# Mean square of the differential heads: from two products over high and low part to one over half-rows

## The chip, the cores and the metric

The kernel runs on one core of a Trainium2 chip. The metric is the device time of one execution in microseconds, and less is better. A core has a matrix engine (TensorE, PE in the profile), a vector engine (VectorE, DVE), a scalar engine (ScalarE, ACT), a general engine (GpSimd, POOL) and a queue that issues most transfers (SyncE, SP). Each engine works through its own queue in order, and waits where an operand that another engine makes is not there yet.

## The reference

One decoder block on 528 positions (16 meta tokens and 512 tokens) of width 1024. After a LayerNorm, one projection of 10,240 columns feeds two attention branches of eight and sixteen heads, their gates and the merge gates. The edited part belongs to the differential branch. For each of its eight heads:

```python
a = p[:, :, 0] - lam * p[:, :, 1]                      # difference of two softmaxes
y = einsum('bhqk,bhkd->bhqd', a, v)                    # 128 channels for each query
xf * lax.rsqrt(jnp.mean(jnp.square(xf), axis=-1, keepdims=True) + RMS_EPS)   # RMS norm over them
```

The norm's result is scaled by the gain and by 0.8, multiplied by a SiLU gate, and goes on into the branch's output projection, the merge, the last projection and the closing LayerNorm.

## The kernel before

Everything is kept transposed: channels stand on the 128 partitions and the 512 tokens along the row. TensorE multiplies in a rounded 32-bit format (F32R). To stay near full precision, each operand is split in a high part (a copy rounded to F32R) and a low part (the rest, again F32R), and a product is taken as high by high, high by low and low by high. ScalarE makes most high parts, VectorE most low parts. A mean over the channels is a mean over partitions, which no vector pass can make, so it is a product with `onesm`, a 128 x 128 matrix whose every element is 1/128 (line 283). 1/128 has no low part, so the mean square takes two products: `onesm` by the high part of the squares and `onesm` by the low part.

The main loop (lines 969 to 1037) goes over 16 units: the eight differential heads, then eight pairs of stick-breaking heads. While one unit's attention runs, the next unit's keys and values and the one after's queries are projected (`proj_tok`, `proj_pos`, `stage_kv`). Each stretch of four input blocks of a weight is loaded, split in high (line 185, ScalarE) and low part (line 190, VectorE) by `prep`, four stretches ahead of the product that uses it, and held in six buffers.

A differential unit runs `d_scores` (scores, line 761; bias and minimum, 841; exponential, 845; difference, 851), then `transposed` (773, 778, 779), then `d_values`, whose products end with line 870. `d_values` also squares the attention output `av`, which lies in a PSUM bank of which there is one, and splits the squares. `d_norm`, called in the next unit at the due time 3.0 (5.8 after the last head; line 994), has the two products into a bank `ms` of the pool `ptp` (two banks, which the transposes use too), then Ln and Exp on ScalarE (lines 888 and 890, together the power -1/2), the multiplication with `av` and the gain on VectorE (893) and a store to DRAM (894). The buffers `sqh`, `sql` and `yd` come from the pool `gpool` under the tag `sg`, which has six buffers of 128 x 512 and is shared with the gates; `sq` and `r` share one buffer.

What sets the order: `run` calls the attention steps between the projection's parts by due times, so the code emits an order. Up to line 967 and from line 1041 on, `keep_order` ties each engine to the emitted order. In the main loop nothing is tied but a few single instructions (`placed`, `behind`, `follow`) and TensorE in the last unit: there the framework's planner sets the order on each engine. It simulates the program in time with its own costs (line 1270) and, where several instructions could go next on an engine, decides by that simulated time and the emitted order. On the chip the order is then fixed.

Of the kernel before, what the change touches and what calls it, by code (L numbers as in the profile page):

```python
# [9 lines left out]
F32 = mybir.dt.float32  # L10
F32R = mybir.dt.float32r
BF16 = mybir.dt.bfloat16
AF = mybir.ActivationFunctionType
ALU = mybir.AluOpType
PSUM = bass.MemoryType.PSUM

P = 128
D = 1024
KT = D // P
S = 512  # L20
# [22 lines left out]
LO, HI = slice(0, 64), slice(64, 128)  # L43
# [3 lines left out]
def hybrid_block_kernel(ctx: ExitStack, tc: tile.TileContext, x, meta, emb_g, emb_b, w_in, b_gate,  # L47
                        diff_lambda, subln_g, w_br_d, w_br_s, w_out, ln_g, ln_b, out):
    nc = tc.nc
    v, s, g, pe = nc.vector, nc.scalar, nc.gpsimd, nc.tensor  # L50
# [10 lines left out]
    gpool = ctx.enter_context(tc.tile_pool(name="g", bufs=6))  # L61
# [154 lines left out]
    def behind(name, on=True):  # L216

        if on:
            ins = nc.cur_bb.bb.instructions[-1]
            if name in state:  # L220
                follow(ins, state[name])
            state[name] = ins
# [22 lines left out]
    start = ExitStack()  # L245
# [37 lines left out]
    onesm = const.tile([P, P], F32R, name="onesm")  # L283
# [299 lines left out]
    with tc.tile_pool(name="att", bufs=1) as ap:  # L583
# [270 lines left out]
        def d_values(unit, ta):  # L854
            vh, vl = unit["V"]
            h, l = [v4[:, 2 * m:2 * m + 2].rearrange("p c d -> p (c d)") for m in range(2)]
            av = pav.tile([P, 512], F32, tag="av", name="av")
            unit["av"] = av
            pe.matmul(av, vh[:, 0, :], ta[0][0], start=True, stop=False)
            pe.matmul(av[:, 3 * P:], v3[:, 0:2].rearrange("p c d -> p (c d)"), ta[3], start=False, stop=False)  # L860
            ends = av.rearrange("p (i q) -> p i q", i=NB)[:, :, 96:]
            pe.matmul(ends, h, ta["strips"], start=False, stop=False)
            pe.matmul(ends, l, ta["strips"], start=False, stop=False)
            for j in range(1, 3):
                o = av[:, j * P:]
                pe.matmul(o, vh[:, j, :], ta[j][0], start=False, stop=False)
                pe.matmul(o, vh[:, j, :], ta[j][1], start=False, stop=False)
                pe.matmul(o, vl[:, j, :], ta[j][0], start=False, stop=False)
            pe.matmul(av, vh[:, 0, :], ta[0][1], start=False, stop=False)
            pe.matmul(av, vl[:, 0, :], ta[0][0], start=False, stop=True)  # L870
            sq = ap.tile([P, S], F32, tag="sq", name="sq")
            s.activation(sq, av, AF.Square)
            sqh = gpool.tile([P, S], F32R, tag="sg", name="sqh")
            sql = gpool.tile([P, S], F32R, tag="sg", name="sql")
            s.copy(sqh, sq)
            v.tensor_tensor(sql, sq, sqh.bitcast(F32), op=ALU.subtract)
            unit["sq"] = sqh, sql

        def d_norm(unit, h):
            av, sq = unit["av"], unit["sq"]  # L880
            ms = ptp.tile([P, 512], F32, tag="tp", name="ms")
            pe.matmul(ms, onesm, sq[0], start=True, stop=False)
            pe.matmul(ms, onesm, sq[1], start=False, stop=True)
            r = ap.tile([P, S], F32, tag="sq", name="r")
            if h == 7:
                s.preload_act_table_set("natural_log_exp_and_others")
                behind("act")
            s.activation(r, ms, AF.Ln, bias=epsr)
            behind("act", h == 7)
            s.activation(r, r, AF.Exp, scale=-0.5)  # L890
            behind("act", h == 7)
            y = gpool.tile([P, S], F32, tag="sg", name="yd")
            v.scalar_tensor_tensor(y, av, g08, r, op0=ALU.mult, op1=ALU.mult)
            nc.sync.dma_start(kept["d"][h], y)
# [74 lines left out]
        for u, (kind, n) in enumerate(UNITS):  # L969
            unit = units[u]  # L970
# [16 lines left out]
            if kind == "d":  # L987
# [3 lines left out]
                parts = transposed(ta, apads[n % 2])  # L991
                steps += [(t0 + 0.7 * m, f) for m, f in enumerate(parts)]
                steps.append((t1, lambda: d_values(unit, ta)))
                pending = [(3.0 if n < 7 else 5.8, lambda unit=unit, n=n: d_norm(unit, n))]
            else:
                if n == 0:
# [31 lines left out]
                for c in range(2):  # L1028
                    ta = {}
                    steps += spread(s_scores(unit, c, n == 0), (2.0 + 4.3 * c) if n == 0 else 4.4 * c, 0.85, 5)  # L1030
                    parts = transposed(ta, apads[c])
# [15 lines left out]
    def operands(y):  # L1047


        gh, gl = [lp.tile([P, 7, 4, 256], F32R, tag=n, name=n) for n in ("gh", "gl")]  # L1050

        def part(i):
            a, b = y[i], y[i + 4]
            t = lp.tile([P, 4, 256], F32, tag="tmp", name="t", bufs=2)
            v.tensor_tensor(t[:, 0, :], a[:, LEFT], a[:, RIGHT], op=ALU.subtract)
            v.tensor_tensor(t[:, 2, :], a[:, RIGHT], b[:, RIGHT], op=ALU.subtract)
            v.tensor_tensor(t[:, 1, :], t[:, 2, :], a[:, LEFT], op=ALU.subtract)
            v.tensor_tensor(t[:, 3, :], t[:, 1, :], b[:, LEFT], op=ALU.add)
            for o, src in ((slice(0, 1), a[:, LEFT].unsqueeze(1)), (slice(1, 3), b.rearrange("p (a n) -> p a n", a=2)),
                           (slice(3, 7), t)):  # L1060
                s.copy(gh[:, o, i, :], src)
                v.tensor_tensor(gl[:, o, i, :], src, gh[:, o, i, :].bitcast(F32), op=ALU.subtract)

        return (gh, gl), [lambda i=i: part(i) for i in range(4)]
# [40 lines left out]
    G, parts = operands(ydT)  # L1105
# [11 lines left out]
    G, parts = operands(ysT)  # L1117
# [75 lines left out]
    for c in range(2):  # L1193
        for t in range(NB):
            st, final = sts[t], t == NB - 1
            for o, w in [(0, 256), (256, 256)] if final and c else [(0, 512)]:
# [5 lines left out]
                for n, (k, (m, w)) in enumerate(products):  # L1202
                    pe.matmul(ps, MH[k][:, ts(t, P)] if m == "h" else ML[:, k, ts(t, P)], WO[c]["hl".index(w)][:, k, r],  # L1203
                              start=(n == 0), stop=(n == 3 * KT - 1))
# [70 lines left out]
```

## Time and profile before

| What | Value |
| --- | --- |
| Median of 3 runs | 706.76 us (706.19 to 706.91) |
| The profiled execution | 706.21 us |
| its span, first to last instruction | 704.4 us |
| TensorE busy | 694.8 us (99%) |
| VectorE busy | 569.9 us (81%) |
| ScalarE busy | 440.7 us (63%) |
| Mean granted TensorE clock | 0.997 |
| First product of the mean square (line 882) | x8, from 79.8 to 258.2 us |
| Second product (line 883) | x8, from 81.9 to 261.7 us |

A row of a time line gives the start in us from the span's start, the duration, the engine, the line of the code, the operation, what it writes and reads, and the shapes. In brackets at the end stands how long the engine had been idle and what ended that. A row of a group gives, behind the bar, the busy time in us, the mean duration of one in ns, and the idle time ahead of them. A row of waits names who waited for what: us in total, how often, the longest. Matmuls are pipelined, and their rows overlap.

### The profile page before, as it was taken

To read this page: it belongs to the slowest core of one execution; us is meant where nothing else is said; L and a number is where in the kernel's file an instruction comes from. 1 tells how busy PE (TensorE), PEld (TensorE's weight loads), DVE (VectorE), ACT (ScalarE), POOL (GpSimd) and SP (SyncE) were. 2 spreads that over 40 slices of the span, in tenths; PEclk is the share of its full clock that TensorE was granted. 3 is DMA by queue.
4 is the path that set the end of the run, shared out by engine and by line. 5 is a ranking of instruction groups with operands and counts; after the bars stand their busy time and mean duration, and the time that the engine had idled before them with its cause. 6 is when DMAs were issued, how large, how long until landed. Compare 5 with 4: busy or idle time off the path is not lost.

```text
span 704.4 us, 13288 instructions
## 1 busy us (share of the span) xinstructions
PE 694.8 (99%) x4482; PEld 635.4 (90%) x4482; DVE 569.9 (81%) x1224; ACT 440.7 (63%) x1071; POOL 131.2 (19%) x144
## 2 busy tenths in 40 slices
PE   9999999999999999999999999999999999999995
PEld 8999999989899898998989899988888998999885
DVE  6887998878786777989877998976666788688886
ACT  5776767767566687777767687766555456555400
POOL 3243112222222201212121220000012101230011
PEclk9999999999999999999999999999999999999998
DMA  9398557988987886899798976647476749697702
GB/s 290 96 197 185 148 115 180 212 177 181 219 189 171 204 191 186 171 220 209 204 192 220 201 158 187 168 119 239 145 168 128 154 122 245 128 186 190 264 33 102
DMA packets 184054, 124.93 MB, mean 177 GB/s; under 512 B 8961, under 2 KB 168098, under 8 KB 183986
## 3 DMA queue, kind: packets, MB, share of 16 engines
q1 hardware_dynamic: 147890, 102.84, 50.1%
q0 software_dynamic: 35776, 20.19, 22.8%
q10 hardware_dynamic: 320, 1.06, 0.4%
q8 instruction: 35, 0.57, 0.3%
q14 instruction: 33, 0.27, 0.1%
HBM read 93.54 MB, written 9.44 MB: 146 GB/s over the span
## 4 chain that ended last, share of the span: by engine, by line
PE 95%; ACT 2%; DVE 1%; DMA 1%; issue 0%; SPq 0%; DVEq 0%; POOL 0%; ACTq 0%
PE q L697 18%; PE ps L498 12%; PE ps L496 12%; PE ps L497 12%; PE q L1080 11%; PE pso L1203 6%; PE ps L512 6%; PE sc L761 6%; PE t L773 4%; PE bank L387 1%; PE tv L730 1%; DMA xt<-in_x_dram 1%; PE av L928 1%; PE av L929 1%; PE av L922 1%; PE av L923 1%
## 5 line engine op out<-in xcount | busy, mean ns | idle before, releaser
L497 PE MATMUL ps<-hTl,w 128*128 128x512 f32 x368 | 144.7, 393 | 0.0
L190 DVE TENSOR_TENSOR w<-raw,w 128x512 fp32r<-128x512 f32 x168 | 114.4, 689 | 37.3 <-ACT w L185 36.5
L496 PE MATMUL ps<-hTh,w 128*128 128x512 f32 x368 | 144.6, 393 | 0.0
L498 PE MATMUL ps<-hTh,w 128*128 128x512 f32 x368 | 144.6, 393 | 0.0
L185 ACT CAST w<-raw 128x512 fp32r<-128x512 f32 x168 | 103.4, 627 | 11.7 <-PE ps L498 5.4
L147 POOL DMA_DIRECT2D rawk<-in_w_in_dram x48 | 66.1, 1631 | 121.6 <-DMA rawk<-in_w_in_dram 55.2
L697 PE MATMUL q<-tS,w 128*128 128x264 f32 x384 | 82.5, 289 | 0.0
L1080 PE MATMUL q<-gh,w 128*128 128x256 f32 x448 | 81.4, 283 | 0.2 <-ACT t L1089 0.2
L498 PEld LDWEIGHTS ps<-hTh,w 128*128 128x128 f32 x368 | 69.2, 188 | 13.6
L497 PEld LDWEIGHTS ps<-hTl,w 128*128 128x128 f32 x368 | 69.2, 188 | 13.1
L496 PEld LDWEIGHTS ps<-hTh,w 128*128 128x128 f32 x368 | 69.2, 188 | 13.0
L1080 PEld LDWEIGHTS q<-gh,w 128*128 128x128 f32 x448 | 70.1, 192 | 0.5 <-ACT t L1089 0.4
L761 PE MATMUL sc<-k,A 128*128 128x264 f32 (+3 forms) x320 | 65.8, 298 | 0.0
L697 PEld LDWEIGHTS q<-tS,w 128*128 128x128 f32 x384 | 63.6, 188 | 0.3
L1080 PE MATMUL q<-gl,w 128*128 128x256 f32 x224 | 63.4, 283 | 0.0
L697 PE MATMUL q<-hTh,w 128*128 128x264 f32 x288 | 60.8, 286 | 0.0
L913 DVE TENSOR_TENSOR_SCAN e<-e,diag 128x528 f32<-128x528 f32 (+1 forms) x64 | 54.2, 851 | 5.6 <-ACT e L907 5.6
L697 PE MATMUL q<-tl,w 128*128 128x264 f32 x192 | 54.8, 286 | 0.0
L761 PEld LDWEIGHTS sc<-k,A 128*128 128x128 f32 x320 | 50.1, 189 | 2.1
L512 PE MATMUL ps<-hTh,w 128*128 128x264 f32 x256 | 51.5, 288 | 0.2 <-ACT k L639 0.2
L697 PEld LDWEIGHTS q<-hTh,w 128*128 128x128 f32 x288 | 47.7, 189 | 1.0 <-DVE kvt L717 0.2
L778 ACT CAST ah<-t 128x384 fp32r<-128x384 f32 (+2 forms) x72 | 34.4, 478 | 22.4 <-PE t L773 22.3
(283 smaller groups left out, 1576.0 us busy)
## 6 DMA issues: line engine op xcount, KB each, us to landing
raw<-in_w_in_dram SPq DMA_DIRECT2D x140, 256.0 KB, 3.5
rawk<-in_w_in_dram POOLq DMA_DIRECT2D x48, 256.0 KB, 5.9
rawk<-in_w_in_dram SPq DMA_DIRECT2D x36, 256.0 KB, 3.7
k<-ks SPq DMA_DIRECT2D x60, 132.0 KB, 3.2
raw<-in_w_out_dram SPq DMA_DIRECT2D x16, 256.0 KB, 3.0
k<-ks SPq DMA_DIRECT2D x60, 66.0 KB, 3.2
A<-low SPq DMA_DIRECT2D x28, 128.0 KB, 2.4
raw<-in_w_br_diff_dram SPq DMA_DIRECT2D x12, 256.0 KB, 5.1
```

Source lines behind the costliest of these rows:

```text
L147: second[l] = [lambda raw=raw, x=x: g.dma_start(raw, x, accum_op=ALU.add) for x in more]
L185: s.copy(wh, raw)
L190: eng.tensor_tensor(wl, raw, wh.bitcast(F32), op=ALU.subtract)
L496: pe.matmul(ps, wh[:, k % 4, :], hTh[:, k, M:], start=(k == 0), stop=False)
L497: pe.matmul(ps, wh[:, k % 4, :], hTl[:, k, M:], start=False, stop=False)
L498: pe.matmul(ps, wl[:, k % 4, :], hTh[:, k, M:], start=False, stop=(k == KT - 1))
L512: pe.matmul(ps[:, :H2], a[:, k % 4, :], b[:, k, ts(c, H2)], start=(k == 0 and m == 0), stop=(k == KT - 1 and m == 2))
L697: pe.matmul(bank, a[:, k, :], b, start=start and k == 0 and j == 0, stop=k == 3 and j == 2, skip_group_check=not start)
L761: pe.matmul(ps[:, :n], q, K[:, m, k0:k0 + n], start=(m == 0), stop=(m == 1))
L913: v.tensor_tensor_scan(rev, rev, diag[0][:, L - nk:][:, ::-1], 0.0, ALU.mult, ALU.max)
L1080: pe.matmul(bank, a[:, k, :], b[:, n, k, :], start=start and k == 0 and m == 0, stop=k == 3 and m == 2, skip_group_check=not start)
L1203: pe.matmul(ps, MH[k][:, ts(t, P)] if m == "h" else ML[:, k, ts(t, P)], WO[c]["hl".index(w)][:, k, r], start=(n == 0), stop=(n == 3 * KT - 1))
```

## The change

The mean over 128 channels is the sum over the lower 64 partitions plus the sum over the upper 64, divided by 128. The new code squares both halves separately, each as a pass over 64 partitions: the lower half into `sq[LO]`, the upper half, moved to the lower partitions, into `half[LO]`. VectorE adds the two. The sums fill only 64 partitions, so their high part and their low part fit into one tile: ScalarE writes the high part into the lower partitions of `parts`, VectorE the low part into the upper ones. One product of `onesm` with that tile adds up all 128 partitions, and so high and low parts together. `d_norm` has one product in place of two. The rest of `d_norm`, its due times and all other code stay.

```diff
-            s.activation(sq, av, AF.Square)
-            sqh = gpool.tile([P, S], F32R, tag="sg", name="sqh")
-            sql = gpool.tile([P, S], F32R, tag="sg", name="sql")
-            s.copy(sqh, sq)
-            v.tensor_tensor(sql, sq, sqh.bitcast(F32), op=ALU.subtract)
-            unit["sq"] = sqh, sql
+            s.activation(sq[LO], av[LO], AF.Square)
+            half = gpool.tile([P, S], F32, tag="sg", name="half")
+            s.activation(half[LO], av[HI], AF.Square)
+            v.tensor_tensor(sq[LO], sq[LO], half[LO], op=ALU.add)
+            parts = gpool.tile([P, S], F32R, tag="sg", name="parts")
+            s.copy(parts[LO], sq[LO])
+            v.tensor_tensor(parts[HI], sq[LO], parts[LO].bitcast(F32), op=ALU.subtract)
+            unit["sq"] = parts
...
-            pe.matmul(ms, onesm, sq[0], start=True, stop=False)
-            pe.matmul(ms, onesm, sq[1], start=False, stop=True)
+            pe.matmul(ms, onesm, sq, start=True, stop=True)
```

## The prediction

> **What bounds the kernel now.** I read the page's busy shares first, then the waits of TensorE, then the stretches, and last the time line around the edited lines.
>
> ```profile
> span 704.4 us, 13288 instructions
> PE 694.8 (99%) x4482; PEld 635.4 (90%) x4482; DVE 569.9 (81%) x1224; ACT 440.7 (63%) x1071; POOL 131.2 (19%) x144
> ```
>
> ```profile
> PE warm L308 <- POOL ident masks.py:199: 1.4, 1, 1.4
> PE bank L341 <- DVE xn L337: 0.2, 1, 0.2
> PE ps L512 <- ACT k L639: 0.2, 1, 0.2
> PE q L1080 <- ACT t L1089: 0.2, 1, 0.2
> ```
>
> ```profile
> 72.00:260.00 188.00, 188.00 (x1268) 174.71 (x1267) 156.25 (x422) 132.09 (x340) 40.49 (x39) 1.00 0.81 180
> ```
>
> The second block lists every wait of TensorE that the view shows in the whole span: us in total, how often, the longest. They come to 2.0 us. The third is the stretch in which all eight differential heads are normed: length, then busy us (and instructions) of PE, PEld, DVE, ACT and POOL, then granted clock, DMA share, GB/s. TensorE is busy for all 188.00 us at clock 1.00, VectorE for 156.25 (83%), ScalarE for 132.09 (70%). So TensorE sets the end, and what leaves its queue should come off the total, unless it is made to wait. What it then gains is not the busy time of a matmul, since a busy row runs into the next one:
>
> ```profile
> 79.61 0.40 PE L496 MATMUL ps<-hTh,w 128*128 128x512 f32 x1
> 79.84 0.39 PE L882 MATMUL ms<-sqh,onesm 128*128 128x512 f32 x1
> 80.07 0.39 PE L497 MATMUL ps<-hTl,w 128*128 128x512 f32 x1
> ...
> 81.66 0.40 PE L498 MATMUL ps<-hTh,w 128*128 128x512 f32 x1
> 81.89 0.39 PE L883 MATMUL ms<-sql,onesm 128*128 128x512 f32 x1
> 82.12 0.39 PE L496 MATMUL ps<-hTh,w 128*128 128x512 f32 x1
> ```
>
> The columns are start and duration. Each of these products is shown as 0.39 us, but the next one starts 0.23 us behind it (81.89 to 82.12). 0.23 us is the place in the queue that a removed product gives back; 0.39 is the length of its pipeline. The rows also show that the two products of one head, emitted one behind the other in the code, stand 2.05 us apart with projection products between: in the main loop the order on TensorE is the planner's.
>
> **The change part by part.** (a) The second product of the mean square (L883) goes, with its weight load, in each of eight heads. By 0.23 us each that is 8 x 0.23 = 1.84 us. By the busy time it would be 8 x 0.39 = 3.1 us, and I reject that: it counts the overlap with the following product twice. The lower bound is nothing, if some other engine becomes the bound; I take 1.84 us, since the rows show the pitch on both sides of both products. The Trainium skill, on the page "TensorE: Matmul & The Clock Gate", section "Back-to-back issue gap", says that in a real stream of weight loads and products one of 512 columns costs about 131 ns, not the isolated 216 ns; the sum would then be 8 x 0.131 = 1.05 us. The 0.23 us between the rows above speaks against it here.
>
> (b) ScalarE gets a third pass per head. The passes and VectorE's now:
>
> ```profile
> L872 ACT ACTIVATE sq<-av 128x512 f32<-128x512 f32 x8 | 4.8, 597 | 4.7 <-PE av L870 4.6
> L875 ACT CAST sqh<-sq 128x512 fp32r<-128x512 f32 x8 | 5.1, 640 | 0.0
> L876 DVE TENSOR_TENSOR sql<-sq,sqh 128x512 fp32r<-128x512 f32 x8 | 6.0, 748 | 0.0
> L935 ACT COPY half<-av 64x512 f32<-64x512 f32 x16 | 9.3, 582 | 12.2 <-PE av L930 8.5 <-issue 2.6 <-ACT e L909 0.9
> L538 ACT COPY gr<-ps 128x512 f32<-128x512 f32 x6 | 3.5, 588 | 0.0
> L353 DVE SCALAR_TENSOR_TENSOR A<-bank,A 64x512 fp32r<-64x512 f32 x4 | 2.8, 690 | 1.8 <-ACT A L349 1.7
> L170 DVE TENSOR_TENSOR rawk<-rawk,raw 128x512 f32<-128x512 f32 x12 | 8.2, 684 | 0.0
> ```
>
> Columns behind the bar: busy us, mean ns of one, idle before. A copy of 64 partitions takes 582 ns against 588 for 128 of them, so halving the height saves nothing: two half Squares cost 2 x 0.59 instead of 0.60, and the cast stays at about 0.64. ScalarE: +0.59 us a head, 4.7 us in all. (c) VectorE gets one addition per head: 0.69 us by L170 and L353 (684 and 690 ns, full and half height), 5.5 us in all; the subtraction stays one of 512 columns. In the 188 us stretch that lifts VectorE from 156.25 to 161.8 and ScalarE from 132.09 to 136.8, against about 186.2 for TensorE then. Both stay below TensorE, so I cost them at nothing. What covers them is that weights are prepared ahead:
>
> ```profile
> ACT w L185 <- PE ps L498: 18.2, 22, 2.1
> ```
>
> ScalarE's weight casts wait for TensorE to give a weight buffer back, 22 times and up to 2.1 us: it is ahead of TensorE, as far as its buffers let it. If that cover went, the price is bounded by 4.7 + 5.5 = 10.2 us when every added pass lay on TensorE's path; nothing in the rows comes near that, since TensorE doesn't wait at all there.
>
> (d) The chain from the attention product to the mean square becomes longer. Before it is Square, cast, subtraction; now Square, Square, addition, cast, subtraction, with three changes of engine instead of one. The first head and the sixth, seventh and eighth, before:
>
> ```profile
> 73.85 0.39 PE L870 MATMUL av<-ah,V 128*128 128x512 f32 x1
> 74.28 0.60 ACT L872 ACTIVATE sq<-av 128x512 f32<-128x512 f32 x1
> 74.78 0.47 ACT L738 CAST V<-tv 128x384 fp32r<-128x384 f32 x1
> ...
> 75.30 0.64 ACT L875 CAST sqh<-sq 128x512 fp32r<-128x512 f32 x1
> ...
> 76.37 0.69 DVE L876 TENSOR_TENSOR sql<-sq,sqh 128x512 fp32r<-128x512 f32 x1
> ```
>
> ```profile
> 199.09 0.68 DVE L876 TENSOR_TENSOR sql<-sq,sqh 128x512 fp32r<-128x512 f32 x1
> 199.75 0.44 PE L882 MATMUL ms<-sqh,onesm 128*128 128x512 f32 x1
> 200.02 0.40 PE L883 MATMUL ms<-sql,onesm 128*128 128x512 f32 x1
> 200.26 0.30 PE L697 MATMUL q<-hTh,w 128*128 128x264 f32 x1
> ```
>
> ```profile
> 227.15 0.68 DVE L876 TENSOR_TENSOR sql<-sq,sqh 128x512 fp32r<-128x512 f32 x1
> 227.81 0.44 PE L882 MATMUL ms<-sqh,onesm 128*128 128x512 f32 x1
> 228.09 0.39 PE L883 MATMUL ms<-sql,onesm 128*128 128x512 f32 x1
> ```
>
> ```profile
> 257.12 0.68 DVE L876 TENSOR_TENSOR sql<-sq,sqh 128x512 fp32r<-128x512 f32 x1
> 258.24 0.39 PE L882 MATMUL ms<-sqh,onesm 128*128 128x512 f32 x1
> ```
>
> In the first head the cast ends at 75.94 and the subtraction starts 0.43 us later: that is what a change of engine costs with the work that is queued between. On ScalarE the next pass starts 0.50 us behind the Square (74.28 to 74.78). By these durations the first head's new chain would run: second Square 74.78 to 75.38, addition 75.81 to 76.50, cast 76.93 to 77.57, subtraction 78.00 to 78.69, with 0.43 us at each change. It ended at 77.06, so it becomes 1.6 us longer. Bounds: with nothing queued at the three changes 77.40, or 0.35 us longer; with 0.86 us at each 79.98, or 2.9 us. I take 1.6, since every engine's queue goes on holding the same other work. In the first head the low part was there at 77.06 and L883 starts at 81.89; 1.6 us more are hidden in those 4.83 us. In the sixth and seventh it is there at 199.77 and 227.83, and L883 starts 0.25 and 0.26 us later: no cover. The product must stand further back there, about 201.4 and 229.4, and TensorE must have something else to do until then. The cast now waits for VectorE's addition; behind it in ScalarE's queue stand the next head's exponentials, projections' evacuations and weight casts, for which VectorE and TensorE wait in turn. Since the planner draws the order anew with the changed passes in it, I take it that it puts the product where it reckons the operand ready, as it did when it set the pair of the first head 2.05 us apart, with both operands there long before. Its cost for TensorE I take as 0.05 us per head at most, 0 in the forecast: in the sixth head the two products now stand at 0.27 and 0.24 us instead of 0.23, so about 0.05 us of wait is in the kernel before already, and may go as well. From below, a loss: waits as in the rivals. From above, a gain of 8 x 0.05 = 0.4 us on top.
>
> (e) The bank of the mean square is held from one product to the Ln, not from the first of two; `parts` is one buffer of the gate pool where two were held until the products, and `half` is free after the addition. That eases two rotations; TensorE waits for neither now, so nothing comes of it. DMAs are untouched: no issue is moved or added, only the store of the normed head follows the chain.
>
> Sum: -1.84 + 0 + 0 + 0 = -1.84 us. The profiled execution took 706.21 us, its span 704.4 with 1.8 us around it, and would take 704.4. It stands 0.55 us below the median of the three runs, 706.76, against which the comparison goes: 706.76 - 1.84 = 704.9 us, 0.26% less. About 0.2%, 1.41 us, is what a measurement of this kernel can tell from no change, so the line lies at 705.35, and the forecast is only 0.4 us on the near side of it.
>
> **The rivals.** *The gain is eaten or smaller (within 0.2%).* TensorE waits a little at the new place of the product: 0.4 to 3.2 us in all eight heads together, 0.05 to 0.4 each. For it: the two heads without cover; if the planner kept L883's place there, TensorE would wait 1.6 - 0.25 = 1.35 us in each, 2.7 in all, and the time is 706.76 - 1.84 + 2.7 = 707.6. Against it: the planner places by readiness. Typical: 1 us of waits, 705.9. The skill's 131 ns ("TensorE: Matmul & The Clock Gate") would land in this case too, at 705.7, without any wait.
>
> *Slower: the product stands in the queue ahead of its operand.* TensorE takes its queue in order, so one product whose operand is late holds all products behind it. If the planner reckons the longer chain shorter than it is, and keeps the place of the first of the pair, TensorE waits 199.77 + 1.6 - 199.75 = 1.6 us in the sixth head, 1.6 in the seventh and 257.80 + 1.6 - 258.24 = 1.2 in the eighth: 4.4 us, and the time is 706.76 - 1.84 + 4.4 = 709.3 (with the bounds of 0.35 and 2.9 us for the chain 705.7 and 713.2). It decides from 0.4 us a head on, 3.25 us in all (1.84 + 1.41). For it: sub-0.3 us margins in these heads. Against it: in the first head the planner was late rather than early, and TensorE has not one listed wait between 72 and 260 us.
>
> *TensorE isn't the bound, the change shows nothing.* The 5.5 us of additions fall on VectorE at its busiest, which then feeds scores and transposes late; each head would lose about what it gains: 706.8. Against it: VectorE at 83%.
>
> **How the numbers follow.** The forecast, 704.3 to 705.35 us: 0.50. Gain eaten, within 0.2% (with the bound on VectorE): 0.29. Slower by the product in its place: 0.21. So faster by over 0.2% 0.50, within 0.29, slower 0.21. The predicted time is the forecast's 704.9. The range goes down to 703.8, which is the forecast with 0.4 us of present waits gone and 0.7 for a luckier order, and up to 708.6, which takes in the rival with 2.7 us of waits and the beginning of the slower one; about 0.18 is left out, two thirds of it above.
>
> **What would show it.** Right: 8 products fewer on TensorE and a pitch of 0.23 us around the one that is left, no new row in TensorE's list of waits between 72 and 260 us, a span of about 702.6, half-height Squares at 0.58 to 0.60 us each, an addition at 0.69, and the stretch from the first head's attention product to the last norm shorter by nearly 2 us with the tail unchanged. Wrong: starts around the mean square's product over 0.3 us apart; the product less than 0.1 us behind the end of the low part in more than two heads, with a gap ahead of it; or a new wait of TensorE elsewhere, on scores, transposes or weight splits, which would mean that the new order and not the product decides.

## The result, and the profile after

The changed kernel takes 712.71 us (median of 5 runs, 712.45 to 714.14), the kernel before 706.74 in the same comparison: ratio 1.009, with a 95% interval of 1.0079 to 1.0101. It is about 6 us slower, above the predicted range (703.8 to 708.6), where 704.9 was forecast.

The page of the changed kernel, its span and busy shares:

```profile
span 710.7 us, 13289 instructions
...
PE 696.6 (98%) x4474; PEld 636.0 (89%) x4474; DVE 576.3 (81%) x1232; ACT 446.1 (63%) x1079; POOL 133.0 (19%) x144
```

TensorE has 8 instructions fewer, as it should, and the span is 6.3 us longer. VectorE gained 6.4 us and ScalarE 5.4; neither is near the span. (In the code after, the passes stand at lines 872, 874, 875, 877 and 878, the product at 884, Ln at 889; other lines of this part are one further down.)

The stretches, first of the changed kernel, then the second one of the kernel before (columns as in the prediction: length, busy us of PE, PEld, DVE, ACT, POOL with counts, clock, DMA share, GB/s):

```profile
72.00:260.00 188.00, 186.51 (x1254) 173.14 (x1253) 162.06 (x429) 137.36 (x346) 42.44 (x39) 1.00 0.81 182
260.00:476.00 216.00, 212.84 (x1352) 193.12 (x1350) 178.42 (x334) 152.85 (x399) 34.24 (x30) 0.99 0.79 184
```

```profile
260.00:476.00 216.00, 216.00 (x1374) 195.95 (x1373) 182.84 (x343) 156.10 (x409) 35.06 (x31) 1.00 0.79 187
```

Where the edited code runs TensorE is idle for 1.5 us of 188; behind it, where not a line was changed, for 3.2 us of 216, and before for none. What it waited for, in the whole span (us in total, how often, the longest):

```profile
PE sc L761 <- issue: 2.3, 1, 2.3
...
PE ps L496 <- DVE kvt L714: 0.9, 1, 0.9
PE q L697 <- ACT gr L538: 0.5, 1, 0.5
PE av L923 <- ACT ys L940: 0.4, 1, 0.4
```

No row names the mean square's product. The largest is a wait of scores (L761) of a stick-breaking pair. To close the sum I took the starts of all TensorE rows, gave each shape the median distance to the next start, and added up what the distances over 60 ns more than that come to:

| From TensorE's first start to its last, us | before | after |
| --- | --- | --- |
| The instructions at their median distances | 683.97 | 682.06 |
| Longer distances, 0 to 240 us | 10.24 | 10.64 |
| 240 to 280 us | 0.52 | 2.48 |
| 280 to 320 us | 0.69 | 4.77 |
| 320 to 480 us | 2.88 | 5.06 |
| 480 us to the end | 1.29 | 1.20 |
| All other differences from the median | -4.46 | -4.31 |
| In all | 695.13 | 701.90 |

The products that are gone gave 1.91 us back, and two thirds of it had arrived at the seventh head, whose last attention product (L870) starts at 223.42 instead of 224.71. The loss comes behind that, in single waits, above all around 310 us.

The place around 310 us, on SyncE (first six rows) and on TensorE of the changed kernel, then SyncE of the kernel before:

```profile
300.63 1.49 SPq L621 DMA_DIRECT2D A<-A  x1
302.21 0.56 SPq L621 DMA_DIRECT2D A<-low  x1
302.87 0.54 SPq L556 DMA_DIRECT2D gd<-yd  x1
307.15 0.46 SPq L621 DMA_DIRECT2D A<-low  x1
307.70 0.55 SPq L651 DMA_DIRECT2D k<-ks  x1
...
310.30 1.28 SPq L650 DMA_DIRECT2D k<-ks  x2
...
309.96 0.60 PE L773 MATMUL t<-ident,apad 128*128 128x128 f32 x4
312.83 0.48 PE L761 MATMUL sc<-k,A 128*128 128x264 f32 x2 [2.27 <-issue]
```

```profile
303.79 1.28 SPq L650 DMA_DIRECT2D k<-ks  x2
305.17 0.56 SPq L621 DMA_DIRECT2D A<-A  x1
305.82 0.66 SPq L621 DMA_DIRECT2D A<-low  x1
```

`k<-ks` are the stores that bring a new unit's keys into place (lines 650 and 651); `A<-A` and `A<-low` assemble the queries of a later unit (line 621). Before, the keys' stores stand ahead of the query transfers in SyncE's queue. Now the query transfers stand in front. The third of them overwrites what the first reads, so it waits until the first has landed, and the six stores behind it in the queue go out late. SyncE's own list of waits between 280 and 320 us has it:

```profile
SPq L621 <- DMA A<-A: 3.7, 1, 3.7
```

The stores go out at 307.70 to 311.58 us, and the scores that read those keys start at 312.83.

The second place, at 256 us, on ScalarE, VectorE and TensorE of the changed kernel:

```profile
253.07 1.28 ACT L887 ACT_TABLE_LOAD   x1
254.37 0.59 ACT L872 ACTIVATE sq<-av 64x512 f32<-64x512 f32 x1
254.98 0.59 ACT L874 ACTIVATE half<-av 64x512 f32<-64x512 f32 x1
...
255.61 0.68 DVE L875 TENSOR_TENSOR sq<-sq,half 64x512 f32<-64x512 f32 x1 [0.46 <-ACT half L874]
...
256.88 0.41 DVE L714 TENSOR_TENSOR kvt<-q,kvt 128x264 f32<-128x264 f32 x1
...
257.35 0.50 PE L496 MATMUL ps<-hTh,w 128*128 128x512 f32 x1 [0.92 <-DVE kvt L714]
```

In the eighth head the load of the activation table now stands ahead of the Squares (before, it stood behind the Square, at 255.13). They come late, VectorE idles for the addition, and behind the addition stands the evacuation L714, the pass that reads out the bank which TensorE needs. Both places point to order: no operation there is longer than it was, though the second has a Square and an addition more.

### The profile page after: what moved, and what is told of

It reads as the page before. It is cut to its first block, busy times and chain, and to the rows that moved or that the text cites. A ratio compares the mean times of both kernels' runs of the same rounds, so it can differ in the third digit from the quotient of the medians.

```text
span 710.7 us, 13289 instructions
## 1 busy us (share of the span) xinstructions
PE 696.6 (98%) x4474; PEld 636.0 (89%) x4474; DVE 576.3 (81%) x1232; ACT 446.1 (63%) x1079; POOL 133.0 (19%) x144
## 4 chain that ended last, share of the span: by engine, by line
PE 86%; ACT 5%; DVE 4%; issue 3%; DMA 1%; POOL 0%; DVEq 0%; SPq 0%; ACTq 0%; POOLq 0%
PE q L697 14%; PE ps L496 11%; PE ps L497 11%; PE ps L498 11%; PE q L1081 11%; PE pso L1204 6%; PE ps L512 6%; PE sc L761 5%; PE t L773 3%; PE bank L387 1%; DVE w L190 1%; PE tv L730 1%; ACT w L185 1%; PE av L929 1%; PE av L930 1%
## 5 line engine op out<-in xcount | busy, mean ns | idle before, releaser
L761 PE MATMUL sc<-k,A 128*128 128x264 f32 (+3 forms) x320 | 67.1, 301 | 2.3 <-issue 2.3
L761 PEld LDWEIGHTS sc<-k,A 128*128 128x128 f32 x320 | 49.9, 189 | 4.9 <-issue 2.5
L941 POOL DMA_DIRECT2D ys<-half x14 | 11.7, 838 | 200.1 <-ACT ys L940 98.7
```

The source lines that it names most:

```text
L761: pe.matmul(ps[:, :n], q, K[:, m, k0:k0 + n], start=(m == 0), stop=(m == 1))
```

## The experiments

Each is compared with the kernel before on the same chip (706.3 to 706.7 us there). Where an order is said to be that of another kernel, a table of instruction numbers for each engine and queue ties each instruction to the one ahead of it, which sets the planner aside. In 1 to 5 the table stands at the top, so that the lines are 61 to 64 higher than in the kernel it comes from; in 13 it stands at the end.

**1. The new passes in the old order.** All operations of the change; every queue as in the kernel before; VectorE's two passes ahead of where the subtraction was, the product at L883's place.

```diff
+    for steps_ in given.values():
+        at, old = 0, None
+        for d in steps_:
+            at += d
+            new = named[f"I-{at}"]
+            if old is not None:
+                follow(new, old)
+            old = new
```

> The changed passes, with the order on all five queues written out as the planner set it for the kernel before: each second Square right behind the first, the addition two instructions ahead of the subtraction, the one product where the second of the pair stood (in the eighth head right ahead of the next transposes). If the new order is what costs (theory O): 706.7 - 1.84 + 2.7 us for the product standing 1.35 us too early in the sixth and seventh head = 707.6, and no wait of TensorE on scores near 310 us. If the added passes themselves cost, whatever the order (theory W): 711 to 713.

Measured: 708.56 us, ratio 1.0031 (1.0021 to 1.0041). Its waits of TensorE in the edited region, and VectorE in the sixth head:

```profile
PE ms L945 <- DVE parts L939: 1.2, 2, 0.6
...
PE q L758 <- ACT gr L599: 0.8, 1, 0.8
```

```profile
199.95 0.68 DVE L939 TENSOR_TENSOR parts<-sq,parts 64x512 fp32r<-64x512 f32 x1
200.67 0.43 DVE L778 TENSOR_TENSOR vT<-kvt,q 128x264 f32<-128x264 f32 x1
```

Where a price is given "by the distances", it is the time between two starts beyond the median, as in the table above; the view's waits are shorter. In the sixth and seventh heads the product waits for the low part, about 0.8 us each by the distances, and the next projections 0.23 more, since L778 (717 in the kernel before), which frees their bank, starts at 200.67 instead of 199.69. In the fifth head the cast holds an evacuation (L599, 538 before) back on ScalarE, 0.95 us. In all, the longer distances between 160 and 240 us grow by 3.3 us. So with the order kept the passes cost more than the product gives. 708.56 is 3.7 us above 706.68 - 1.84; the changed kernel is 7.8 us above the same kind of sum. The longer chain has a price of its own where the order was made for the shorter one, and that is less than half of what happened.

**2. The same with the product 12 matmuls further back** in the first to seventh heads. The edit is another table.

> As the run before it, but the product stands twelve matmuls further back (1.5 to 2.7 us), so that the longer chain is covered. Theory O: 704.9 to 705.6, that is the gain forecast. Theory W: 711 to 713.

Measured: 709.78 us, ratio 1.0042 (1.0027 to 1.0057): a miss. The product no longer waits, the projections behind do:

```profile
PE q L758 <- DVE vT L778: 1.1, 1, 1.1
PE q L758 <- DVE kvt L778: 1.1, 1, 1.1
```

With the product out of the way, the evacuation that stands behind the two new passes on VectorE ends last. It was there all the time, hidden by the product's wait. Moving the product alone gives nothing back. (That 2 is above 1 is mostly a wait of 0.7 us at 495 us, far behind the edit; the two intervals overlap.)

**3. The old passes in the new order.** The code of before, its instructions in the order that the changed kernel has, the two products next to each other at the one's place.

> The passes of the kernel before (one Square, cast, subtraction, two products), with the order on all queues as the planner set it for the changed kernel; the cast stands in the place of the second Square and in the first four heads the subtraction stands three to five instructions further ahead, because a buffer's turn asks for it; the pair stands where the one product stood. Theory O: 712.7 + 1.84 less about 1.1 us for the eighth head, where no addition holds VectorE any more: 712 to 714.5, slower than before although its passes are the same. Theory W: 706.7 to 707.5.

Measured: 713.73 us, ratio 1.0097 (1.008 to 1.0114). Without one new pass, and with both products, the kernel is 7.0 us slower than before and has the changed kernel's largest waits:

```profile
PE sc L825 <- DMA k<-ks: 2.6, 1, 2.6
...
PE ps L560 <- DVE kvt L778: 0.7, 1, 0.7
PE q L761 <- ACT gr L602: 0.5, 1, 0.5
```

L825 is 761: the scores wait for the keys' stores, and here the view names them. The order alone makes the kernel slow, whether the old work is done in it or the new. Two smaller waits of the changed kernel, at 226 and 250 us, 0.4 and 0.5 us by the distances, are down to 0.13 and 0.15 us here: these two come with the passes.

**4. The changed kernel with the keys' stores ahead of the query transfers.** Ten entries of SyncE's queue are put as before; all other queues keep the changed kernel's order. By lines, the queue becomes:

```diff
- L621 L621 L556 L621 L651 L650 L651 L651 L650 L650
+ L651 L556 L650 L651 L651 L650 L650 L621 L621 L621
```

> The changed kernel in its own order, but for ten neighbouring entries of SyncE's queue: the six stores of the second stick-breaking unit's keys stand ahead of the three transfers of a later unit's queries, as in the kernel before. If the wait of 2.3 us on the scores at 310 us comes from the third query transfer, which waits for the first and holds the keys' stores behind it: that wait is gone and 712.7 - 2.3 = 710.4. If something else holds the scores: 712.7, unchanged.

Measured: 708.83 us, ratio 1.0027 (1.0016 to 1.0038). That is 3.9 us less than the changed kernel, more than the 2.3 expected: the longer distances between 280 and 320 us fall from 4.77 to 0.77 us, so those behind the wait (about 1 us at 314 to 317 us) came from it too. Nearly two thirds of the loss of 6 us hang on these ten entries.

**5. And the table load behind the eighth head's passes as well.** ScalarE's queue, by lines, the other passes between them left out:

```diff
- L887 L872 L874 L877
+ L872 L874 L877 L887
```

> The changed kernel with its planner's order, in which two places are put as in the kernel before: the ten entries of SyncE's queue (keys' stores ahead of query transfers), and the table load that stands ahead of the eighth head's Squares on ScalarE, which goes behind the head's passes. Theory (the wait of 1.08 us of the key projections at 256 us comes from the table load, which delays the Squares, the addition and the evacuation behind it on VectorE): 708.83 less about 1.1, 707.7, and no wait for an evacuation (kvt, L714) near 256 us. Rival (that wait belongs to the longer chain itself, as in the sixth and seventh heads under the old order): 708.8, the wait still there or at the mean square's product. Seen beside 712.7 for the changed kernel and 706.5 for the kernel before.

Measured: 708.06 us, ratio 1.0021 (1.0012 to 1.003). The wait is half as long (0.53 instead of 1.08 us by the distances), and 0.8 us of the expected 1.1 come back (0.6 against the kernel before of each comparison; the intervals of 4 and 5 overlap, so the trace carries this more than the times):

```profile
PE ps L560 <- DVE kvt L778: 0.4, 1, 0.4
```

The addition now starts at 255.14 with VectorE busy up to it, and the evacuation at 256.41 instead of 256.88. So the table load is about half of that wait. What the other half hangs on was not separated; 3, which has no addition there, still waits 0.7 us. The rest of the loss is in smaller waits whose causes I did not take apart. By the distances the changed kernel has them at 226 us (0.4 us), 250 (0.5), 381 (0.7) and 475 to 477 (1.4 in three).

**6. One product alone.** The kernel before without L883. The low part is left out of the mean, so it shows what the product's place is worth, and is no version to use.

```diff
-            pe.matmul(ms, onesm, sq[0], start=True, stop=False)
-            pe.matmul(ms, onesm, sq[1], start=False, stop=True)
+            pe.matmul(ms, onesm, sq[0], start=True, stop=True)
```

> The kernel before with the second product of each mean square left out, so that the low part of the squares does not enter the mean (this leaves out that part of the computation); all passes as before, order left to the planner. If a removed product gives back its pitch of 0.23 us: 706.7 - 8 x 0.23 = 704.9. If the product was worth nothing there: 706.7; by the busy time of 0.39 us it would be 703.6.

Measured: 709.23 us (707.67 to 711.62), ratio 1.0038 (1.0023 to 1.0053): a miss on the other side. Work is taken away, nothing is added, and the kernel is slower. SyncE, TensorE's wait, and SyncE's longest wait between 325 and 342 us:

```profile
320.77 8.24 SPq L145 DMA_DIRECT2D raw<-in_w_in_dram  x3
...
330.62 0.47 SPq L621 DMA_DIRECT2D A<-A  x1
...
334.42 0.53 SPq L621 DMA_DIRECT2D A<-low  x1
...
337.14 0.58 SPq L621 DMA_DIRECT2D A<-low  x1
...
338.17 1.28 SPq L650 DMA_DIRECT2D k<-ks  x2
```

```profile
PE sc L761 <- DMA k<-ks: 1.7, 1, 1.7
```

```profile
SPq L145 <- DVE w L190: 6.3, 1, 6.3
```

In the next stick-breaking unit, too, query transfers stand between the keys' stores, the last two of which go out from 338.17 on, and the scores wait. But no query transfer is listed as waiting for the landing of another here. What held the queue longest was a weight load (L145): three stand ahead of the stores (the row of 8.24 us), where the kernel before has two, and the third waits 6.3 us for VectorE to give its buffer back. The kernel before has all its stores there first:

```profile
328.57 1.44 SPq L651 DMA_DIRECT2D k<-ks  x2
...
335.26 0.51 SPq L621 DMA_DIRECT2D A<-A  x1
```

**7. The passes alone.** The kernel before, with a half Square and a half addition into a buffer that nothing reads.

```diff
+            spare = gpool.tile([P, S], F32, tag="sg", name="spare")
+            s.activation(spare[LO], av[HI], AF.Square)
+            v.tensor_tensor(spare[LO], sq[LO], spare[LO], op=ALU.add)
```

> The kernel before with a second half-height Square and a half-height addition added in each head, into a buffer that nothing reads; cast, subtraction and both products stay, order left to the planner. Theory O (only the new order costs, and it comes from the longer chain that the product waits for): 706.7 to 707.2. Theory W (the added passes hold VectorE and ScalarE where TensorE depends on them): 708.7 to 710.5, with waits of TensorE near 172, 200 and 229 us.

Measured: 711.84 us, ratio 1.0073 (1.0049 to 1.0096). Its two largest new waits are again the keys' stores (in the same unit as in 6, behind the same weight load), and the mean square's product in the eighth head:

```profile
PE sc L761 <- DMA k<-ks: 2.4, 1, 2.4
...
PE ms L885 <- DVE v L751: 0.7, 1, 0.7
```

**8, 9, 10. One product alone, the passes alone, and the whole change, with one rule for SyncE:** a query transfer follows the eight keys' stores that the code emitted last ahead of it. The planner sets everything else.

```diff
                 nc.sync.dma_start(o.bitcast(F32), src.bitcast(F32))
+                for key in state.get("keys", []):
+                    follow(nc.cur_bb.bb.instructions[-1], key)
...
             staged.clear()
+            state["keys"] = [i for i in nc.cur_bb.bb.instructions[-8:] if i.engine == mybir.EngineType.SP]
```

> The run with one product alone (the low part left out of the mean), and one rule more for the planner: a unit's query transfers are queued on SyncE behind all stores of the keys emitted ahead of them. If the 1.7 us of wait for keys at 339 us hid the gain of the product (theory: the product gives its pitch, the queue took it back): 704.9 to 705.6. If a removed product is worth nothing: 706.7 to 707.5.

> The run with the added passes alone, with the same rule for SyncE's queue. If only the queue costs: 706.7. If the passes have a price of their own, by holding VectorE and ScalarE in the sixth to eighth head: 711.8 less 2.5 us of wait for keys and about 1 us behind it = 708.3.

> The changed kernel with the same rule for SyncE's queue, the rest left to the planner. The wait for keys near 310 us must be gone: 708.8 as with the ten entries set by hand, or between 706.5 and 709 if the planner draws another order with it. If the rule doesn't matter: 712.7.

| | planner's order | with the rule | ratio to before (interval) |
| --- | --- | --- | --- |
| one product alone | 709.23 | 706.87 | 1.0004 (0.9995 to 1.0013) |
| the passes alone | 711.84 | 709.41 | 1.0038 (1.0023 to 1.0053) |
| the whole change | 712.71 | 708.62 | 1.0028 (1.0018 to 1.0038) |

The rule gives 2.4, 2.4 and 4.1 us (the kernel before came out 0.2 to 0.4 us lower in the comparison with the rule, so 2.1, 2.2 and 3.7 against it). For the whole change it does what the ten entries did: every engine's order is the changed kernel's, only SyncE's queue differs, and its list of waits has no keys in it. For one product alone the forecast is missed by 1.3 us or more: 1.1 us of waiting for keys is left at 338 us even so, and with it the kernel comes out even with before. The weight load that waits 6.3 us is still ahead of the stores there, so the place of the query transfers is only 0.6 us of the 1.7 in that wait; what else the rule changed in the time was not told apart. The passes alone come out 1.1 us above what was expected, and 0.7 us of waiting for keys is left in them too.

**11, 12. The change in heads 1 to 7, and in head 8 alone;** the other heads as before, the planner's order.

```diff
+            if head < 7:
                 s.activation(sq[LO], av[LO], AF.Square)
...
+            else:
+                s.activation(sq, av, AF.Square)
```

> The change in the first seven heads, the eighth as before; order left to the planner. If the eighth head's longer chain, which ends among the first steps of the stick-breaking units, is what upsets the order (theory O8): 706.7 - 7 x 0.23 + 0.5 to 1.5 us of waits in the sixth and seventh head = 705.6 to 706.6, keys' stores ahead of queries' transfers. If each changed head costs alike: 706.7 + 7/8 x 6 = 712.

> The change in the eighth head alone; order left to the planner. Theory O8: most of the loss is there, 706.7 - 0.23 + 5 to 7 us = 711 to 713.5, with a wait of TensorE on scores of some 2 us near 310 us. If each changed head costs alike: 706.7 + 1/8 x 6 = 707.5.

Measured: 705.48 us for heads 1 to 7, ratio 0.998 (0.997 to 0.999), faster than before; 710.76 for head 8 alone, ratio 1.0053 (1.0038 to 1.0068). SyncE in the first:

```profile
303.37 2.23 SPq L650 DMA_DIRECT2D k<-ks  x2
305.69 0.56 SPq L621 DMA_DIRECT2D A<-A  x1
```

At this place the order on SyncE is the old one again. Head 8 alone has one Square and one addition more and one product less than the kernel before. Its keys come late, and twice:

```profile
PE sc L761 <- DMA k<-ks: 2.9, 2, 1.9
```

So in this pair the change in the eighth head, the last before the stick-breaking units, turns the order over. Seven heads of eight are a gain when it does not.

**13. The old order with the chain further back.** As 1, but in the fifth to seventh heads VectorE's addition and subtraction stand behind the evacuation L717 (in the fifth the addition moves up to it, and only the subtraction goes back), the cast one or two passes further back on ScalarE and the product 8 to 20 matmuls; the Ln moves too. The four were moved together.

> The changed passes in the order of the kernel before, as in the first of these runs, but in the fifth, sixth and seventh head the chain stands out of the way: addition and subtraction behind the subtraction that frees a bank of the keys' projection (line 717), the cast two passes later on ScalarE, the product 8 to 20 matmuls later. If the waits of 0.95, 1.0 and 1.0 us at 172, 200 and 229 us come from where the chain's passes stand in VectorE's and ScalarE's queues: 708.6 - 2.9 = 705.4 to 706.0, faster than the kernel before. If the added work itself is too much for VectorE there: 707.5 to 708.6, with the waits further on.

Measured: 705.24 us (705.07 to 706.19), ratio 0.9982 (0.9973 to 0.9992). VectorE and TensorE in the sixth head:

```profile
198.53 0.42 DVE L717 TENSOR_TENSOR vT<-kvt,q 128x264 f32<-128x264 f32 x1
198.86 0.68 DVE L875 TENSOR_TENSOR sq<-sq,half 64x512 f32<-64x512 f32 x1
...
200.33 0.68 DVE L878 TENSOR_TENSOR parts<-sq,parts 64x512 fp32r<-64x512 f32 x1
...
201.51 0.40 PE L884 MATMUL ms<-parts,onesm 128*128 128x512 f32 x1
201.75 0.41 PE L697 MATMUL q<-hTh,w 128*128 128x264 f32 x2
```

The low part is there at 201.01, the product starts 0.5 us behind it, and the next one 0.24 us behind the product. No wait of TensorE between 72 and 476 us is left in the list. The whole change, in an order that suits it, beats both kernels: 1.1 us below before, 7.5 below the change as the planner ordered it. Against 1 it shows that the 3.3 us there were a matter of what stands behind the new passes, not of the passes' work.

## Why the prediction was wrong

(a) *Eight products at 0.23 us each, 1.84 us.* Right. The product that is left has the same distance:

```profile
232.00 0.40 PE L498 MATMUL ps<-hTh,w 128*128 128x512 f32 x1
232.24 0.39 PE L884 MATMUL ms<-parts,onesm 128*128 128x512 f32 x1
232.47 0.39 PE L496 MATMUL ps<-hTh,w 128*128 128x512 f32 x1
```

The instructions at their median distances came to 1.91 us less. By the 131 ns of the Trainium skill ("TensorE: Matmul & The Clock Gate", "Back-to-back issue gap") the estimate was 1.05 us; these rows, 0.23 to 0.24 us apart, go against that figure here.

(b) *The passes' durations.* Right: half Squares of 0.59 us, an addition of 0.68. In the stretch from 72 to 260 us VectorE came to 162.06 us (161.8 predicted), ScalarE to 137.36 (136.8).

(c) *The passes cost nothing, since VectorE is busy for 83%.* Wrong for three heads, when the order is kept. 83% is a mean over 188 us. In the sixth and seventh heads the bank that TensorE needs next is freed by a VectorE pass that stood directly behind the subtraction, and 0.7 us more ahead of it go through to TensorE (1 and 2); in the fifth it is freed by a ScalarE pass behind the cast, which waited for the addition. With the chain out of their way it cost nothing that the list shows (13). The price depended on what was queued behind, which the prediction named in general and did not look up. In the changed kernel the passes cost about 0.6 us at 226 and 250 us, the part that is gone in 3.

(d) *The chain is 1.6 us longer; the planner puts the product where the operand is ready; cost 0.* From the last attention product to the end of the low part the chain became 0.4 to 4.3 us longer in the changed kernel, 2.0 in the mean, and 0.7 to 1.5 us, 1.0 in the mean, with the old order; 1.6 lies between, though the first head's 4.3 is outside the stated bound of 2.9. The planner did put the product behind its operand: in every head it starts at least 1.6 us after the low part's end, and never waits. But "cost 0" was drawn from the product alone. To place it the planner drew the whole order anew, and 3 prices that order, without any of the change's work, at 7.0 us. Here the prediction failed. Its last paragraph had named the sign, a new wait on scores or weight splits "which would mean that the new order and not the product decides", but no term of the sum was given to it, and of the range 0.7 us downward, for a luckier order, and nothing upward.

(e) *"DMAs are untouched: no issue is moved or added."* Wrong, and the largest single term: none was added, but query transfers moved ahead of keys' stores on SyncE, 3.9 us by 4 and 3.7 to 4.1 by the rule in 10. That the queue goes by the planner too stood in the description of the kernel.

*The slower rival* came near in size (709.3 predicted, up to 713.2) for another reason. Its mechanism, the product ahead of its operand in the sixth to eighth heads, exists in 1, with 0.8 us in each of two heads instead of 1.6, 1.6 and 1.2 in three, and not in the changed kernel; that the size came near is luck. *VectorE as the bound* held only at the places under (c). *Gain eaten* had the right idea of waits, at the wrong place.

In one line: 706.7 before, less 1.9 for the products, plus 4.0 by the keys' stores, 0.6 to 0.8 by the table load; what is left to 712.7, about 3 us, is small waits from 200 us on, at the places named under 5. What causes each was not told apart. What also stays open is why the planner turns the two groups of transfers over when the eighth head's chain grows: 11 and 12 say which head, 6 says that one product less in each head can disturb it too, and no run looked into the planner's reasons.

## What to carry to other kernels

Where a planner sets the order, a sum over the edited operations holds only for the old order: any edit, even one that only takes an instruction away (6), has the order as a second term, here 7 us against 1.9. Tell the two apart by running the old work in the new order and the new work in the old one, and give the forecast's range the room for it beforehand. Look in the queues for a transfer that must wait for another one in front of transfers that the matrix engine needs soon, and tie that order down before tuning passes.

## What was not expected of the hardware

SyncE's queue was held up as a whole by one transfer that had to wait for the landing of another: after the second query transfer (302.21) and one more issue at 302.87 the next went out at 307.15, and six independent stores behind it went out late. In 6 to 9 a weight load that waited 6.3 us for VectorE held the same queue. The ten runs of 6 lie within 3.95 us, those of 13, without a wait for keys, within 1.12; but 12, which waits for keys twice, lies within 0.97 in its four runs, so what makes 6 scatter is open.

The removed products showed in full in no run. The best, 13, has 1.1 us of the 1.8; by the distances 1.0 us went into longer gaps around the changed heads (160 to 280 us: 2.48 us against 1.44 before), none of which is a row in its list of waits.
